# A decoder trunk in fp32 on one core: the sums of the seven-product steps get other homes in SBUF

## The chip, the cores and the metric

The kernel runs on one core of a Trainium2 chip. The metric is device time in microseconds (us). The engines named below are PE (matrix products into PSUM), DVE and ACT (elementwise work), POOL (elementwise work and the accumulating DMAs) and SP (which issues most DMAs).

## The reference

The reference is one layer of a hybrid decoder: RMS norm, one input projection, retention heads and mLSTM heads, an output projection, and then a gated ConvFFN with a final norm. Only the ConvFFN's second half is touched here:

```python
    u = rmsnorm(h, norm_ffn)
    up = causal_dwconv(u @ w_up.astype(u.dtype), ffn_conv_w, ffn_conv_b)
    gate, val = jnp.split(up, [FFN_DIM], axis=-1)
    return h + (jax.nn.silu(gate) * val) @ w_down.astype(h.dtype)
...
    h = rmsnorm(h, norm_final)
    return h[:, N_META:]
```

There are 256 tokens, a model width of 2048 and an inner width of 5632. Everything is float32.

## The kernel before

**Products.** PE takes each float32 operand as two parts: `whi`, a rounded copy that ACT makes (the cast in L121 or L764), and `wlo`, the rest, a subtraction on DVE (L123 or L766). A product is three matmuls: hi x hi, hi x lo and lo x hi.

**Halves.** The inner width is cut into two halves of 22 blocks of 128. For each half the kernel first runs the up projection: block by block two products (gate and value), then a convolution of three taps (`conv3`: `cu` in L680, three terms, the tiles `gt` and `vt`), silu and the product (L788). The results are kept split in `mh`/`ml` (plain steps) and `sh`/`sl` (fast steps). Then follows the down stage: 11 steps q of 256 inner rows, once for the first pair of column blocks of 512 (b = 0) and once for the second pair (b = 2).

**Plain steps and sevens.** Steps 0, 4, 9 and 10 are plain: per column block one load of raw weights (`load_w`, L118), a cast, a subtraction, and 12 matmuls of 128x512. The others are sevens: the two token blocks and two column blocks make a 2x2 product that is done with seven products instead of eight. A seven reads one block `kept`, made ahead of time, and three raw blocks (`wd7`) into one of two homes in `hT` (L840, L841); DVE makes three sums, two in `ta` (L844) and one in `tb` (L845); each is split (L764, L766); 21 matmuls follow (L859 to L862).

**The ring of raw weights.** `wraw` is a ring of 4 tiles of 4 KB per partition in the pool `wpool`. Each plain load takes one of its tiles, and each seven takes two, one for `ta` and one for `tb` (of which half is used). A tile comes free when its `wlo` has been made.

**Where b = 0 gives way to b = 2.** The sevens' results lie in four PSUM tiles `mmps`, the plain ones' and some of the sevens' in four tiles `atps` (`cs`). After the last seven of b, `share` puts `mmps` together: ACT copies p1 to x1 (L884), and DVE makes x6, x7, x6 again and x5 (L886, L887, L889, L895). Four DMAs on POOL's queue (L878, in `onto`) add x1, x7, x6 and x5 to the blocks (0, b), (1, b), (0, b+1) and (1, b+1) of `hn`. After the last step ACT copies the four `cs` tiles (L951) to x tiles, in the order (0, b), (1, b), (0, b+1), (1, b+1), and four more DMAs add these to the same blocks of `hn`. The x tiles are x_tile(0) to x_tile(4): x6, x7, x5 and x1 are tiles 0 to 3; the four copies go to tiles 4, 3, 1 and 0. So the second copy overwrites x1, the third x7 and the fourth x6, each once its accumulate has landed. The next pair's `cs` tiles are the same PSUM banks in the same order, so b = 2's matmuls into its n-th tile (L827 first) wait for the n-th copy.

**What sets the order.** The program is written as loops; a scheduler puts each engine's instructions in order, by its own estimates of times and by when tiles come free. Each engine runs its own list in that order. The pools `wk2` (`cu`, `gt`, `vt`; two buffers of the latter two) and `up` are given up before half 1's down stage, and the pool `more` is opened over their place.

Of the kernel before, what the change touches and what calls it, by code (L numbers as in the profile page):

```python
# [10 lines left out]
F32 = mybir.dt.float32  # L11
F32R = mybir.dt.float32r
AF = mybir.ActivationFunctionType
ALU = mybir.AluOpType
PSUM = bass.MemoryType.PSUM

P = 128
DM = 2048
KT = DM // P
SEQ = 256  # L20
# [9 lines left out]
NF = FFN // P  # L30
# [53 lines left out]
def trunk(ctx: ExitStack, tc: tile.TileContext, io, out: bass.AP):  # L84
    nc = tc.nc

    def pool(name, bufs, **kw):
        return tc.tile_pool(name=name, bufs=bufs, **kw)

    consts = ctx.enter_context(pool("consts", 1, side="left"))  # L90
    wpool = ctx.enter_context(pool("wpool", 1, side="left"))
# [10 lines left out]
    def pcol(name, i, n=1):  # L102
        a = _COLS[name][0]
        return par[:, a + i : a + i + n]
# [34 lines left out]
    def project(src, xh, xl, t0, ps=None):  # L139

        if ps is None:
            ps = mm.tile([P, 512], F32, name="mmps")
        for half in range(2):
            half_tile(ps[:, : xh(0).shape[1] - t0], src, half, xh, xl, t0)
        return ps
# [60 lines left out]
    with pool("sq", 1, side="right") as sqp:  # L206
        for k0, k1 in [(0, 1), (1, 2)] + [(k, k + 2) for k in range(2, KT, 2)]:
            n = k1 - k0
# [3 lines left out]
            raw = wpool.tile([P, 2, W0], F32, name="wraw", bufs=4)[:, :n, :]  # L212
# [5 lines left out]
            for k in range(k0, k1):  # L218
                nc.scalar.activation(xh[:, k, :], hT[:, k, :], AF.Copy, scale=pcol("gmix", k))
                nc.vector.scalar_tensor_tensor(out=xl[:, k, :], in0=hT[:, k, :], scalar=pcol("gmix", k),  # L220
                                               in1=xh[:, k, :].bitcast(F32), op0=ALU.mult, op1=ALU.subtract)
# [47 lines left out]
    with tc.issue_after(parted.ins):  # L269
        a = _COLS["retn"][0]  # L270
        nc.vector.tensor_scalar(out=norms[:, :RH], in0=par[:, a : a + RH], scalar1=-0.5, scalar2=None, op0=ALU.mult)

        a = _COLS["mln"][0]
# [295 lines left out]
    wk2 = wk2_cm.__enter__()  # L569
# [27 lines left out]
    S1, S2, S3, S4, A11, A12, A22 = range(7)  # L597
# [55 lines left out]
    def norm2():  # L653
        ms2 = at.tile([P, 512], F32, name="atps")
        nc.tensor.matmul(ms2[:, :NQ], inv_dm, ssq, start=True, stop=True)
        r0, rt = x_tile(0), x_tile(1)
        r = rsqrt_m2(r0, rt, ms2[:, :NQ], NQ, squared)
        nc.vector.tensor_scalar(out=rstd2, in0=r[:, :NQ], scalar1=-0.5, scalar2=None, op0=ALU.mult)
# [8 lines left out]
    def x_tile(i):  # L667
        return x5[:, i, :]
# [5 lines left out]
        for t in range(2):  # L674
            nc.vector.transpose(dst[:, :, t, 32 * i : 32 * (i + 1)], src[:, :, t, a, :])

    def conv3(ps, f, name):
        u = wk2.tile([P, NQ], F32, name="cu", bufs=1)
        nonlocal evacuated
        evacuated = nc.vector.tensor_tensor(out=u, in0=ps[:, :NQ], in1=rstd2, op=ALU.mult)  # L680
        o = wk2.tile([P, SEQ], F32, name=name)
        nc.scalar.activation(o, u[:, 2:], AF.Identity, scale=pcol("fw", 3 * f + 2), bias=pcol("fb", f))
        for j in range(2):
            nc.vector.scalar_tensor_tensor(out=o, in0=u[:, j : j + SEQ], scalar=pcol("fw", 3 * f + j), in1=o, op0=ALU.mult, op1=ALU.add)
        return o
# [6 lines left out]
    def squares(tt, i, c0, c1):  # L692

        nc.scalar.activation(junk[:, : c1 - c0], hn[:, tt, c0:c1], AF.Square, scale=DM ** -0.5, accum_out=ss4[:, tt, i : i + 1])
# [49 lines left out]
    for half in range(2):  # L744
# [18 lines left out]
        def split(hi, lo, x, after=None):  # L763
            copied = nc.scalar.copy(hi, x)  # L764
            with tc.issue_after(after.ins) if after else nullcontext():
                return copied, nc.vector.tensor_tensor(out=lo, in0=x, in1=hi.bitcast(F32), op=ALU.subtract)  # L766

        gt = None
        for jj in range(NHF):
            j = half * NHF + jj  # L770
            pair = []
            for s in range(2):
                pair.append(project(io["wu"][2 * j + s], uh, ul, 0))
                if j == 0 and s == 0:
                    norm2()
                for e in running:
                    e.age += 1
                if running and running[0].age == 2:
                    running.pop(0).finish(evacuated)
                if 2 * jj + s in begins:  # L780
                    n = begins.index(2 * jj + s)
                    b, q = units[n]
                    running.append(Early(b, half * NQD + q, homes[n], gt, pace))
                    early[b, q] = running[-1].kept
            gt = conv3(pair[0], j, "gt")
            vt = conv3(pair[1], NF + j, "vt")
            nc.scalar.activation(gt, gt, AF.Silu)
            nc.vector.tensor_tensor(out=gt, in0=gt, in1=vt, op=ALU.mult)  # L788
            q, i = divmod(jj, 2)
            if q in PLAIN:  # L790
                k = 2 * PLAIN.index(q) + i
                copied, parted = split(mh[:, k, :], ml[:, k, :], gt)
            elif i == 0:
                f = FAST.index(q)
                even = gt
                copied, parted = split(sh[:, f, A11, :], sl[:, f, A11, :], gt[:, 0:P])
            else:
                e11, e21, e12, e22 = even[:, 0:P], even[:, P:], gt[:, 0:P], gt[:, P:]
                if half == 1 and q in BOTH:
                    split(*(a[:, BOTH.index(q), :] for a in a21), e21)  # L800
                sums = x_tile(0).rearrange("p (a t) -> p a t", a=4)
                nc.gpsimd.tensor_tensor(out=sums[:, S1, :], in0=e21, in1=e22, op=ALU.add)
                nc.gpsimd.tensor_tensor(out=sums[:, S3, :], in0=e11, in1=e21, op=ALU.subtract)
                nc.gpsimd.tensor_tensor(out=sums[:, S2, :], in0=sums[:, S1, :], in1=e11, op=ALU.subtract)
                nc.gpsimd.tensor_tensor(out=sums[:, S4, :], in0=e12, in1=sums[:, S2, :], op=ALU.subtract)
                split(sh[:, f, A12:, :], sl[:, f, A12:, :], gt.rearrange("p (a t) -> p a t", a=2))
                copied, parted = split(sh[:, f, 0:4, :], sl[:, f, 0:4, :], sums)
            if 2 <= j < 18:
                with tc.issue_after(parted.ins):
                    transposed_h((j - 2) // 4, (j - 2) % 4)  # L810
# [21 lines left out]
        def seven(b, q, cs, ps, first, last, after, norm):  # L832


            nonlocal turn
            f = FAST.index(q)
            raw = left[turn]
            turn = 1 - turn

            nc.sync.dma_start(raw[:, 0, :], early[b, q])  # L840
            nc.sync.dma_start(raw[:, 1:4, :], io["wd7"][b // 2, half * NQD + q][:, 1:4, :])  # L841
            ta, tb = (wpool.tile([P, 2, 512], F32, name="wraw", bufs=4) for _ in range(2))

            nc.vector.tensor_tensor(out=ta, in0=raw[:, 0:1, :].to_broadcast([P, 2, 512]), in1=raw[:, 1:3, :], op=ALU.subtract)  # L844
            nc.vector.tensor_tensor(out=tb[:, 0, :], in0=raw[:, 3, :], in1=raw[:, 0, :], op=ALU.subtract)  # L845
            copied = None
            for w, to in (
                (raw[:, 2:4, :], ((S4, cs[0, 1], False, False), (A12, cs[0, 0], False, False))),
                (raw[:, 0:2, :], ((S2, ps[2], first, last), (A11, ps[0], first, last))),
                (ta, ((S3, ps[1], first, last), (S1, ps[3], first, last))),  # L850
                (tb[:, 0:1, :], ((A22, cs[1, 0], False, False),)),
            ):
                hi = wpool.tile([P, 2, 512], F32R, name="whi", bufs=5)
                lo = wpool.tile([P, 2, 512], F32R, name="wlo", bufs=5)
                n = len(to)
                with tc.issue_after(after.ins) if first and after else nullcontext():
                    copied, _ = split(hi[:, :n, :], lo[:, :n, :], w)
                for i, (m, o, begin, _) in enumerate(to):
                    nc.tensor.matmul(o, sh[:, f, m, :], hi[:, i, :], start=begin, stop=False)  # L859
                    nc.tensor.matmul(o, sl[:, f, m, :], hi[:, i, :], start=False, stop=False)  # L860
                for i, (m, o, _, end) in enumerate(to):
                    nc.tensor.matmul(o, sh[:, f, m, :], lo[:, i, :], start=False, stop=end)  # L862
            if norm:

                with tc.issue_after(copied.ins):
                    for g in norm:
                        squares(*g)
                reached = nc.gpsimd.tensor_tensor(out=junk[:, 0:1], in0=tb[:, 0, 0:1], in1=tb[:, 0, 0:1], op=ALU.add)
                with tc.issue_after(reached.ins):
                    for tt, _, c0, c1 in norm:  # L870
                        times_gain(tt, c0, c1)
# [30 lines left out]
        if half == 1:  # L902
# [3 lines left out]
            more = more_cm.__enter__()  # L906
            gfin = more.tile([P, DM], F32, name="gfin", bufs=1)
            nc.gpsimd.dma_start(gfin, io["gfin"])
            junk = more.tile([P, 512], F32, name="junk", bufs=1)
# [7 lines left out]
        for b in (0, 2):  # L917
            cs = {}
# [3 lines left out]
            ps = [mm.tile([P, 512], F32, name="mmps") for _ in range(4)]  # L922
# [38 lines left out]
        if half == 1:  # L961
# [10 lines left out]
            for i in range(2):  # L972
                p = at.tile([P, 512], F32, name="atps")[:, 0:256]
# [95 lines left out]
```

## Time and profile before

| | us |
|---|---|
| median of 3 runs | 1208.73 (1208.54 to 1211.33) |
| profiled execution | 1207.7 |
| its span | 1205.9 |
| PE busy in the span | 1194.6 |
| DVE busy | 971.5 |
| ACT busy | 709.5 |
| POOL busy | 162.8 |

Times in rows count from the start of the span. Half 0's down stage runs from 718 to some 830 us, half 1's from 1084 to the end. In both, b = 0 gives way to b = 2 at the step where L951 stands: at 773 and at 1140 us. A row of the timeline gives the start, the length, the engine, the line, the operation with its tiles, and in brackets how long the engine had been idle and what released it. A row of waits gives who waited for whom: microseconds in total, times, the longest.

### The profile page before, as it was taken

To read this page: it belongs to the slowest core of one execution; us is meant where nothing else is said; L and a number is where in the kernel's file an instruction comes from. 1 tells how busy PE (TensorE), PEld (TensorE's weight loads), DVE (VectorE), ACT (ScalarE), POOL (GpSimd) and SP (SyncE) were. 2 spreads that over 40 slices of the span, in tenths; PEclk is the share of its full clock that TensorE was granted. 3 is DMA by queue.
4 is the path that set the end of the run, shared out by engine and by line. 5 is a ranking of instruction groups with operands and counts; after the bars stand their busy time and mean duration, and the time that the engine had idled before them with its cause. 6 is when DMAs were issued, how large, how long until landed. Compare 5 with 4: busy or idle time off the path is not lost.

```text
span 1205.9 us, 22794 instructions
## 1 busy us (share of the span) xinstructions
PE 1194.6 (99%) x8956; PEld 1151.2 (95%) x8956; DVE 971.5 (81%) x1444; ACT 709.5 (59%) x963; POOL 162.8 (14%) x223
## 2 busy tenths in 40 slices
PE   9999999999999999999999999999999999999997
PEld 9999999999999999999999998878999999998886
DVE  8968788766775966789889879897788778789897
ACT  8747656655656646555555557664555555556664
POOL 0100001111110311021122100202022112100232
PEclk9999999999999999999999999999999999999999
DMA  8765555666565965766766834959787777755956
GB/s 278 269 212 164 170 184 170 197 183 192 169 192 165 349 200 175 252 220 212 253 219 214 279 117 175 278 177 276 284 251 255 223 240 249 261 176 211 274 181 186
DMA packets 83004, 263.27 MB, mean 218 GB/s; under 512 B 14672, under 2 KB 18896, under 8 KB 82768
## 3 DMA queue, kind: packets, MB, share of 16 engines
q1 hardware_dynamic: 71952, 223.85, 57.0%
q0 software_dynamic: 10368, 37.11, 10.1%
q8 instruction: 70, 1.15, 0.4%
q10 hardware_dynamic: 576, 0.85, 0.2%
q14 instruction: 38, 0.31, 0.1%
HBM read 243.42 MB, written 11.27 MB: 211 GB/s over the span
## 4 chain that ended last, share of the span: by engine, by line
PE 96%; DMA 2%; DVE 1%; ACT 0%; issue 0%; SPq 0%; DVEq 0%; ACTq 0%
PE mmps L130 26%; PE mmps L131 25%; PE mmps L133 25%; PE atps L827 2%; PE atps L828 2%; PE atps L830 2%; PE mmps L860 2%; PE mmps L862 2%; PE mmps L859 2%; PE atps L862 1%; PE atps L860 1%; PE atps L859 1%; DMA hn<-x 1%; PE atps L379 1%; DMA hT<-in_wd 1%; PE atps L371 0%
## 5 line engine op out<-in xcount | busy, mean ns | idle before, releaser
L121 ACT CAST whi<-wraw 128x1024 fp32r<-128x1024 f32 x352 | 369.3, 1050 | 342.0 <-PE mmps L131 228.7
L123 DVE TENSOR_TENSOR wlo<-wraw,whi 128x1024 fp32r<-128x1024 f32 x352 | 432.3, 1230 | 72.5 <-ACT whi L121 70.0
L130 PE MATMUL mmps<-uh,whi 128*128 128x258 f32 x1408 | 346.1, 283 | 0.0
L131 PE MATMUL mmps<-ul,whi 128*128 128x258 f32 x1408 | 346.0, 283 | 0.0
L130 PEld LDWEIGHTS mmps<-uh,whi 128*128 128x128 f32 x1408 | 267.6, 190 | 0.1
L131 PEld LDWEIGHTS mmps<-ul,whi 128*128 128x128 f32 x1408 | 267.1, 190 | 0.1
L130 PE MATMUL mmps<-xh,whi 128*128 128x272 f32 (+2 forms) x864 | 219.8, 288 | 0.0
L131 PE MATMUL mmps<-xl,whi 128*128 128x272 f32 (+2 forms) x864 | 218.3, 286 | 0.0
L133 PE MATMUL mmps<-uh,wlo 128*128 128x258 f32 x1408 | 196.5, 282 | 0.0
L133 PEld LDWEIGHTS mmps<-uh,wlo 128*128 128x128 f32 x1408 | 179.9, 189 | 0.0
L131 PEld LDWEIGHTS mmps<-xl,whi 128*128 128x128 f32 x864 | 162.8, 188 | 0.0
L130 PEld LDWEIGHTS mmps<-xh,whi 128*128 128x128 f32 x864 | 162.5, 188 | 0.1
L133 PE MATMUL mmps<-xh,wlo 128*128 128x272 f32 (+2 forms) x864 | 126.7, 285 | 0.0
L133 PEld LDWEIGHTS mmps<-xh,wlo 128*128 128x128 f32 x864 | 114.2, 188 | 0.0
L680 DVE TENSOR_TENSOR cu<-mmps,rstd 128x258 f32<-128x258 f32 x88 | 37.4, 425 | 55.3 <-PE mmps L133 54.8
L764 ACT CAST whi<-hT 128x1024 fp32r<-128x1024 f32 x52 | 53.6, 1052 | 27.2 <-PE atps L828 7.3
L766 DVE TENSOR_TENSOR wlo<-hT,whi 128x1024 fp32r<-128x1024 f32 x52 | 62.1, 1220 | 4.9 <-ACT whi L764 3.7
L131 PE MATMUL mmps<-mixl,whi 128*128 128x258 f32 x256 | 63.0, 283 | 0.0
L130 PE MATMUL mmps<-mixh,whi 128*128 128x258 f32 x256 | 62.4, 282 | 0.0
L764 ACT CAST whi<-wraw 128x1024 fp32r<-128x1024 f32 (+1 forms) x52 | 43.0, 838 | 16.8 <-PE mmps L860 6.8
L766 DVE TENSOR_TENSOR wlo<-wraw,whi 128x1024 fp32r<-128x1024 f32 (+1 forms) x52 | 52.2, 1037 | 0.6 <-PE mmps L862 0.2
L827 PE MATMUL atps<-whi,mh 128*128 128x512 f32 (+1 forms) x132 | 50.9, 387 | 1.3 <-ACT whi L121 1.1
(280 smaller groups left out, 1700.1 us busy)
## 6 DMA issues: line engine op xcount, KB each, us to landing
wraw<-in_wu SPq DMA_DIRECT2D x176, 512.0 KB, 4.4
wraw<-in_wi SPq DMA_DIRECT2D x108, 512.0 KB, 4.1
hT<-in_wd SPq DMA_DIRECT2D x26, 768.0 KB, 4.7
wraw<-in_wd SPq DMA_DIRECT2D x36, 512.0 KB, 4.7
wraw<-in_wo SPq DMA_DIRECT2D x32, 512.0 KB, 4.2
x<-in_wd POOLq DMA_DIRECT2D x13, 768.0 KB, 7.0
hn<-x POOLq DMA_DIRECT2D x27, 256.0 KB, 7.9
hT<-kept SPq DMA_DIRECT2D x26, 256.0 KB, 2.9
```

The source lines that it names most:

```text
L121: nc.scalar.copy(hi, raw)
L123: nc.vector.tensor_tensor(out=lo, in0=raw, in1=hi.bitcast(F32), op=ALU.subtract)
L130: nc.tensor.matmul(ps, hi[:, k, :], xh(kk), start=kk == first, stop=False)
L131: nc.tensor.matmul(ps, hi[:, k, :], xl(kk), start=False, stop=False)
L133: nc.tensor.matmul(ps, lo[:, k, :], xh(kk), start=False, stop=kk == last)
L680: evacuated = nc.vector.tensor_tensor(out=u, in0=ps[:, :NQ], in1=rstd2, op=ALU.mult)
L764: copied = nc.scalar.copy(hi, x)
L766: return copied, nc.vector.tensor_tensor(out=lo, in0=x, in1=hi.bitcast(F32), op=ALU.subtract)
L827: nc.tensor.matmul(ps, ah[i], hi[:, i, cols], start=first and i == 0, stop=False)
L859: nc.tensor.matmul(o, sh[:, f, m, :], hi[:, i, :], start=begin, stop=False)
L860: nc.tensor.matmul(o, sl[:, f, m, :], hi[:, i, :], start=False, stop=False)
L862: nc.tensor.matmul(o, sh[:, f, m, :], lo[:, i, :], start=False, stop=end)
```

## The change

In half 0 a seven takes one tile of the ring, for `ta`. `tb` goes to a tile `both`, which holds what used to be `gt` and `vt` side by side, also with two buffers. In half 1 `ta` and `tb` go to tiles of their own in the pool `more`, with two buffers each (12 KB more in all), and a seven takes nothing from the ring.

```diff
-    def conv3(ps, f, name):
+    def conv3(ps, f, o):
...
-        o = wk2.tile([P, SEQ], F32, name=name)
...
-            gt = conv3(pair[0], j, "gt")
-            vt = conv3(pair[1], NF + j, "vt")
+            both = wk2.tile([P, 2, SEQ], F32, name="both")
+            gt = conv3(pair[0], j, both[:, 0, :])
+            vt = conv3(pair[1], NF + j, both[:, 1, :])
...
-            ta, tb = (wpool.tile([P, 2, 512], F32, name="wraw", bufs=4) for _ in range(2))
+            if half == 0:
+                ta = wpool.tile([P, 2, 512], F32, name="wraw", bufs=4)
+                tb = wk2.tile([P, 2, SEQ], F32, name="both").rearrange("p a t -> p (a t)")
+            else:
+                ta, tb = more.tile([P, 2, 512], F32, name="ta"), more.tile([P, 512], F32, name="tb")
...
-            nc.vector.tensor_tensor(out=tb[:, 0, :], in0=raw[:, 3, :], in1=raw[:, 0, :], op=ALU.subtract)
+            nc.vector.tensor_tensor(out=tb, in0=raw[:, 3, :], in1=raw[:, 0, :], op=ALU.subtract)
...
-                (tb[:, 0:1, :], ((A22, cs[1, 0], False, False),)),
+                (tb.rearrange("p (a n) -> p a n", a=1), ((A22, cs[1, 0], False, False),)),
...
-                reached = nc.gpsimd.tensor_tensor(out=junk[:, 0:1], in0=tb[:, 0, 0:1], in1=tb[:, 0, 0:1], op=ALU.add)
+                reached = nc.gpsimd.tensor_tensor(out=junk[:, 0:1], in0=tb[:, 0:1], in1=tb[:, 0:1], op=ALU.add)
```

Lines from L764 on have other numbers now: L844, L845 are L848, L849; L878 is L882; L884, L886, L887, L889, L895 are L888, L890, L891, L893, L899; L951 is L955. Since the scheduler sees other tiles, it also puts instructions in another order. Three places follow.

POOL, where b = 0 gives way to b = 2 in half 0: the eight accumulates into `hn`, with the semaphores that each waits for. DMASW stands for the landing of an earlier DMA of POOL, Activation for a copy on ACT, DVE for a result of share. Before:

```order
L878 DMA hn<-x_5849 128x512 [waits DVE_49,Activation_49]
L878 DMA hn<-x_5849 128x512 [waits DVE_49]
L878 DMA hn<-x_5849 128x512 [waits DVE_49,Pool_49]
L878 DMA hn<-x_5849 128x512 [waits DVE_49]
L878 DMA hn<-x_5849 128x512 [waits DMASW4_49,Activation_49]
L878 DMA hn<-x_5849 128x512 [waits DMASW5_49,Activation_49]
L878 DMA hn<-x_5849 128x512 [waits DMASW6_49,Activation_49]
L878 DMA hn<-x_5849 128x512 [waits DMASW7_49,DMASW3_49,Activation_49]
```

and now:

```order
L882 DMA hn<-x_5849 128x512 [waits DVE_49,Activation_49]
L882 DMA hn<-x_5849 128x512 [waits DVE_49]
L882 DMA hn<-x_5849 128x512 [waits DMASW4_49,Activation_49]
L882 DMA hn<-x_5849 128x512 [waits DMASW5_49,Activation_49]
L882 DMA hn<-x_5849 128x512 [waits DVE_49,Pool_49]
L882 DMA hn<-x_5849 128x512 [waits DVE_49]
L882 DMA hn<-x_5849 128x512 [waits DMASW0_49,Activation_49]
L882 DMA hn<-x_5849 128x512 [waits DMASW3_49,DMASW1_49,Activation_49]
```

Before, x1, x7, x6 and x5 come first (the first four rows) and the four copies' accumulates after them. Now the first two copies' accumulates stand third and fourth, each waiting for a landing (x1's and x7's), and x6 and x5 behind them. In half 1 the eight rows have moved in the same way.

DVE, half 1, from the splits of b = 0's last seven to x5. Here `ta`, `tb` and `wraw<-hT` are sums of sevens, `wlo<-wraw` by L123 the splits of plain steps, and `x<-mmps` the rows of share. Before:

```order
L766 TENSOR_TENSOR wlo<-wraw,whi 128x512
L123 TENSOR_TENSOR wlo<-wraw,whi 128x1024 x2
L886 TENSOR_TENSOR x_5849<-mmps,x_5849 128x512
L887 TENSOR_TENSOR x_5849<-mmps,x_5849 128x512
L889 TENSOR_TENSOR x_5849<-x_5849,mmps 128x512
L895 TENSOR_TENSOR x_5849<-x_5849,mmps 128x512
```

and now:

```order
L765 TENSOR_TENSOR wlo<-tb,whi 128x512
L848 TENSOR_TENSOR ta<-hT 128x1024
L849 TENSOR_TENSOR tb<-hT 128x512
L123 TENSOR_TENSOR wlo<-wraw,whi 128x1024 x3
L890 TENSOR_TENSOR x_5849<-mmps,x_5849 128x512
L123 TENSOR_TENSOR wlo<-wraw,whi 128x1024
L848 TENSOR_TENSOR ta<-hT 128x1024
L849 TENSOR_TENSOR tb<-hT 128x512
L891 TENSOR_TENSOR x_5849<-mmps,x_5849 128x512
L123 TENSOR_TENSOR wlo<-wraw,whi 128x1024 x2
L893 TENSOR_TENSOR x_5849<-x_5849,mmps 128x512
L899 TENSOR_TENSOR x_5849<-x_5849,mmps 128x512
```

x7 (L887, now L891) stood two rows behind the splits of step 9; now the sums of two later sevens and two more splits of plain steps stand ahead of it. In half 0 it is the same with one `ta`, one `tb` and two splits.

SP, half 0, the loads for the second pair from step 3's seven to step 6's. Before:

```order
L840 DMA hT<-kept_3_7228 128x512
L841 DMA hT<-in_wd 128x1536
L840 DMA hT<-kept_5_7514 128x512
L841 DMA hT<-in_wd 128x1536
L118 DMA wraw<-in_wd 128x1024 x2
L840 DMA hT<-kept_6_7806 128x512
```

and now:

```order
L840 DMA hT<-kept_3_7219 128x512
L841 DMA hT<-in_wd 128x1536
L840 DMA hT<-kept_5_7503 128x512
L118 DMA wraw<-in_wd 128x1024 x2
L841 DMA hT<-in_wd 128x1536
L840 DMA hT<-kept_6_7793 128x512
```

The two loads of plain step 4 (L118) have moved ahead of the L841 row of step 5's seven, and they no longer wait for a tile that a seven holds.

## The prediction

> **What bounds the kernel now.** I read the head of the page first, then what PE waits for over the whole span, then ten-microsecond windows of the two down stages.
>
> ```profile
> span 1205.9 us, 22794 instructions
> PE 1194.6 (99%) x8956; PEld 1151.2 (95%) x8956; DVE 971.5 (81%) x1444; ACT 709.5 (59%) x963; POOL 162.8 (14%) x223
> ```
> ```profile
> PE atps L827 <- ACT whi L121: 1.1, 2, 0.7
> ...
> PE atps L827 <- ACT x L951: 0.2, 1, 0.2
> ```
> ```profile
> 790.00:800.00 10.00, 9.55 (x42) 7.52 (x41) 10.00 (x11) 6.42 (x7) 0.00 (x0) 1.00 0.55 206
> ...
> 810.00:820.00 10.00, 9.35 (x41) 7.38 (x40) 9.91 (x11) 5.30 (x6) 0.00 (x0) 1.00 0.33 109
> ...
> 1140.00:1150.00 10.00, 9.84 (x44) 8.08 (x44) 8.34 (x9) 8.82 (x12) 3.50 (x4) 1.00 1.01 235
> ```
> PE has work 99% of the span. In the down stages it waits three times: twice for the cast of a plain step's weights (L121) and once for a copy that empties a PSUM tile (L951). The windows show the price (columns: time, length, then busy time of PE, PEld, DVE, ACT, POOL): 0.45, 0.65 and 0.16 us are missing. Measured as the start to start of matmuls over their usual 0.23 us, the gaps come to 0.7, 0.9 and 0.4 us, because the matmul after each gap is slower too. So nothing in these stages can win more than 2.0 us. A loss has no such limit, so the places to look at are those where PE has little margin.
>
> **The gain: two weight loads come earlier.** The two L121 waits belong to steps 4 and 9 of half 0's second pair of column blocks (b = 2). Their loads sit in SP's queue until a seven gives back its ring slots:
>
> ```profile
> 783.43 0.42 SPq L841 DMA_DIRECT2D hT<-in_wd  x1
> 788.90 0.93 SPq L118 DMA_DIRECT2D wraw<-in_wd  x2
> ```
> The load of step 4 is issued at 788.9, although the row ahead of it is done at 783.9. With one slot per seven, SP has these two loads directly behind the L840 row of that moment, with no wait on a tb: some 5 us earlier, against a wait of 0.7. Step 9's pair likewise waits for the sums of a seven earlier. I count both gaps as gone: -0.7 - 0.9 = -1.6 us. Instruction counts are unchanged on every engine; tb's subtraction and its split cost the same in another tile.
>
> **The loss: the order on POOL where b = 0 gives way to b = 2.** Here the scheduler has moved more than the diff says. At this place POOL issues eight accumulating DMAs into hn: four from share (x1, x7, x6, x5) and four from the copies of the PSUM tiles, each of which must wait for the share's accumulate into the same block of hn. Before, share's four stand together:
>
> ```profile
> 763.86 0.92 POOL L878 DMA_DIRECT2D hn<-x  x1 [83.33 <-ACT x L884]
> 766.03 2.77 POOL L878 DMA_DIRECT2D hn<-x  x3 [1.25 <-DVE x L887]
> 773.79 3.52 POOL L878 DMA_DIRECT2D hn<-x  x4 [4.99 <-ACT x L951]
> ```
> ```profile
> 1129.28 0.88 POOL L878 DMA_DIRECT2D hn<-x  x1 [44.04 <-ACT x L884]
> 1131.13 2.76 POOL L878 DMA_DIRECT2D hn<-x  x3 [0.96 <-DVE x L887]
> ```
> Now the order on POOL is x1, x7, then the copies' accumulates into blocks (0, b) and (1, b), and only then x6 and x5. The one into (1, b) waits for x7 to land, and x6 stands behind it in the queue. The fourth copy (L951, L955 now) writes the tile that x6 is read from, so it waits for x6 to land; and b = 2's fourth PSUM tile is free only after that copy. A chain of two landings in a row has come into being: x7's DMA, landing, one POOL issue, x6's DMA, landing, copy, PE. That POOL does hold its queue for a landing shows in its waits, once in this run:
>
> ```profile
> POOL hn L878 <- DMA hn<-x: 1.4, 1, 1.4
> ```
> [...]
>
> Besides, x7 itself is made later. Its DVE row (L887, now L891):
>
> ```profile
> 764.25 0.68 DVE L886 TENSOR_TENSOR x<-mmps,x 128x512 f32<-128x512 f32 x1
> 765.03 0.69 DVE L887 TENSOR_TENSOR x<-mmps,x 128x512 f32<-128x512 f32 x1
> ...
> 768.55 1.23 DVE L844 TENSOR_TENSOR wraw<-hT 128x1024 f32<-128x1024 f32 x1
> 769.69 2.35 DVE L123 TENSOR_TENSOR wlo<-wraw,whi 128x1024 fp32r<-128x1024 f32 x2
> ```
> ```profile
> 1076.17 1.22 DVE L844 TENSOR_TENSOR wraw<-hT 128x1024 f32<-128x1024 f32 x1
> ...
> 1080.26 0.69 DVE L845 TENSOR_TENSOR wraw<-hT 128x512 f32<-128x512 f32 x1
> ...
> 1084.79 1.22 DVE L766 TENSOR_TENSOR wlo<-wraw,whi 128x1024 fp32r<-128x1024 f32 x1
> ...
> 1127.08 2.36 DVE L123 TENSOR_TENSOR wlo<-wraw,whi 128x1024 fp32r<-128x1024 f32 x2 [0.44 <-PE atps L862]
> 1129.36 0.69 DVE L886 TENSOR_TENSOR x<-mmps,x 128x512 f32<-128x512 f32 x1
> 1130.13 0.69 DVE L887 TENSOR_TENSOR x<-mmps,x 128x512 f32<-128x512 f32 x1
> ```
> A row of 128x1024 takes 1.14 us from start to start (768.55 to 769.69), one of 128x512 about 0.6 (0.69, less the same overlap). In half 0 a tb, two splits and a ta now stand ahead of x7 behind the two splits of step 9: 0.6 + 3 x 1.14 = 4.0 us. So x7's DMA goes out at 766.0 + 4.0 = 770.0. In half 1 two ta, two tb and two splits more stand ahead of it: 4 x 1.14 + 2 x 0.6 = 5.8, less the idle 0.44: 5.3. To that comes a lead that DVE loses at the start of half 1: ta, tb and ta's split of the first seven (1076.17, 1080.26, 1084.79; 2.9 us together) ran there before the last convolution was done, and now stand behind it. Bounds: none of it is still felt (5.3), or all of it (8.2). DVE has only some 0.8 us of idle time in view to absorb it, so I take 2.1, and x7's DMA goes out at 1131.1 + 7.4 = 1138.5.
>
> When PE needs the tiles, and what a copy takes:
>
> ```profile
> 776.50 0.39 PE L827 MATMUL atps<-whi,mh 128*128 128x512 f32 x1
> ...
> 777.87 0.39 PE L827 MATMUL atps<-whi,mh 128*128 128x512 f32 x1
> ```
> ```profile
> 1140.19 0.50 PE L827 MATMUL atps<-whi,mh 128*128 128x512 f32 x1 [0.16 <-ACT x L951]
> ...
> 1144.42 0.39 PE L827 MATMUL atps<-whi,mh 128*128 128x512 f32 x1
> ```
> ```profile
> 772.92 2.25 ACT L951 COPY x<-atps 128x512 f32<-128x512 f32 x4
> ```
> PE starts b = 2's fourth tile at 777.87 and at 1144.42. The copy is 0.6 us. With L for the landing of x7 and M for that of x6, 0.9 for the POOL issue between them (0.92 for one above), 0.6 for the copy and 0.1 for the hand-overs, PE can go on at 771.6 + L + M in half 0 and 1140.1 + L + M in half 1. The stalls are **L + M - 6.3** and **L + M - 4.3**.
>
> Landings, from asking for the issue to hn at 763.9, at 766.0, at 773.8, at 1131.1 and at 1140.4, and the page's median:
>
> ```profile
> DMA to landing us min/median/max: 8.2/8.2/8.2
> ...
> DMA to landing us min/median/max: 7.1/7.1/7.1
> ...
> DMA to landing us min/median/max: 4.4/4.4/4.4
> ...
> DMA to landing us min/median/max: 6.1/6.1/6.1
> ```
> ```profile
> hn<-x POOLq DMA_DIRECT2D x27, 256.0 KB, 7.9
> ```
> ```profile
> 760.48 4.21 SPq L118 DMA_DIRECT2D wraw<-in_wd  x4
> 778.53 0.33 SPq L840 DMA_DIRECT2D hT<-kept  x1
> ...
> 1125.73 15.53 SPq L118 DMA_DIRECT2D wraw<-in_wd  x6
> ```
> The ones that go out beside weight loads take 7 to 8 us (8.2 at 763.9 and at 1131.1, 7.1 at 766.0); the one at 773.8, where SP issues nothing from 764.7 to 778.5, takes 4.4. In half 0 x7 at 770.0 falls into that lull: L = 5.0, and M = 5.1, a little over the 4.4 because two more go out with it. Stall 3.8 us; bounds 2.5 (4.4 twice) and 8.1 (7.1 and 7.3). In half 1 SP issues loads until 1141.3, so L = 8.2 as x7's own row there; x6 at 1147.6 comes after them: M = 5.5. Stall 9.4; bounds 2.4 (4.4 twice, x7 only 5.3 late) and 13.1 (8.2, 8.4, x7 8.2 late).
>
> [...]
>
> Other moves cost nothing as far as I can walk them: half 1's first seven has its ta cast about 2 us before PE wants it, and behind the last copy the first cast (1.05 us) ends within the six matmuls (1.4 us) that PE still has.
>
> **Sum.** 3.8 + 9.4 - 1.6 = +11.6 us. Against the profiled execution's own 1207.7 (span 1205.9 and 1.8 around it) that is 1219.3. The median of the runs is 1.0 higher, so I predict **1220 us**.
>
> **Rivals.** *The accumulates stay hidden.* If L + M is under 6.3 in half 0 and under 4.3 in half 1, no copy is late, the change does just what it says, and the time is 1208.7 - 1.6 = 1207.1, not slower. For it: 0.2 us is all that copies cost PE now. Against it: every landing quoted is 4.4 or more, so half 1 would have to land both in less than one takes today. 5%. [...] 3%. *Landings as long as beside loads, in both halves*: 8.1 + 13.1 - 1.6 = +19.6, 1228; decided if the issue at 770.0 takes over 7 us. 15%. *DVE's lost lead stalls PE as well at the start of half 1*: if ta's cast there comes over 2 us later than I walk it, PE waits up to the 2.9 us that were moved, 1223. 10%. *My chain, 1213 to 1225*: 65%. The remaining 2% is for a gain that I do not see.
>
> **How the numbers follow.** The bounds give 2.5 + 2.4 - 1.6 = +3.3 and 8.1 + 13.1 - 1.6 = +19.6, or 1212 to 1228; I take 1213 to 1229, since casts behind the copies have only 0.3 us of margin and can add something at the upper end. A change of 0.3%, 3.6 us, is about what a measurement here tells from none. Slower by more: 15 + 10 + 65 = 0.90. Within it, the first two rivals: 0.08. Faster: 0.02, since PE's gaps hold only 2.0 us.
>
> **What would show it.** In the profile after: PE waits for copies of L955 in both halves, before the third and fourth tile of b = 2, of 2 to 8 us in half 0 and 5 to 13 in half 1; POOL's x6 accumulate goes out some 8 us after x7's instead of 1; the two L121 waits are gone; POOL waits for its own hn<-x. I am wrong if POOL shows share's four accumulates together, or if PE has no wait on L955, or if landings in these places are under 4 us.

## The result, and the profile after

The changed kernel takes 1225.0 us in the median (1224.09 to 1226.85), the kernel before 1209.4 beside it (1208.54 to 1211.33): a ratio of 1.0138, with a 95% interval of 1.0126 to 1.015. The change makes the kernel some 16 us slower. The profiled execution took 1226.85 us, 19.15 more than the profiled one before; that is the pair of executions which the accounting below splits up, and it lies 3.5 us further apart than the medians.

The head of the page:

```profile
span 1225.1 us, 22795 instructions
PE 1200.4 (98%) x8956; PEld 1154.1 (94%) x8956; DVE 969.2 (79%) x1444; ACT 706.2 (58%) x963; POOL 167.3 (14%) x223
```

DVE and ACT are busy a little less than before, POOL 4.5 us more, which is still only 14% of the span. PE is busy for 5.8 us more with the same 8956 matmuls, so some of them were slower. The rest of the 19 us has to be waiting. What PE and POOL wait for (us in total, times, the longest):

```profile
PE atps L827 <- ACT x L955: 10.4, 4, 3.7
...
PE mmps L866 <- DVE wlo L765: 0.3, 1, 0.3
```
```profile
POOL hn L882 <- DMA hn<-x: 12.0, 5, 4.8
```

The two waits for a plain step's cast (L121) are gone. In their place PE waits 10.4 us for the copies out of PSUM (L955, formerly L951, 0.2 us), and POOL holds its queue for 12.0 us until its own accumulates have landed (1.4 before). POOL's row of issues shows where, in half 0 and in half 1:

```profile
773.25 0.88 POOL L882 DMA_DIRECT2D hn<-x  x1 [6.31 <-DVE x L891]
775.41 0.86 POOL L882 DMA_DIRECT2D hn<-x  x1 [1.28 <-ACT x L955]
776.99 2.63 POOL L882 DMA_DIRECT2D hn<-x  x3 [0.72 <-DMA hn<-x]
782.88 0.86 POOL L882 DMA_DIRECT2D hn<-x  x1 [3.25 <-DMA hn<-x]
...
1144.44 0.88 POOL L882 DMA_DIRECT2D hn<-x  x1 [6.96 <-DVE x L891]
1146.25 0.85 POOL L882 DMA_DIRECT2D hn<-x  x1 [0.93 <-ACT x L955]
1151.88 2.61 POOL L882 DMA_DIRECT2D hn<-x  x3 [4.78 <-DMA hn<-x]
```

The first row of each is x7, the second the copies' accumulate into (0, b), the group of three the one into (1, b) with x6 and x5 behind it. In half 1 x7 is issued at 1144.44, and after one more issue POOL stands still until it has landed. x6, which has nothing to do with that landing, goes out some 8 us after x7 instead of one. ACT's copies wait for both landings in turn:

```profile
1145.38 1.06 ACT L955 COPY x<-atps 128x512 f32<-128x512 f32 x2
1151.45 0.58 ACT L955 COPY x<-atps 128x512 f32<-128x512 f32 x1 [5.00 <-DMA hn<-x]
1156.79 0.58 ACT L955 COPY x<-atps 128x512 f32<-128x512 f32 x1 [4.75 <-DMA hn<-x]
```

And PE behind them, in its own rows of both halves:

```profile
775.17 0.50 PE L827 MATMUL atps<-whi,mh 128*128 128x512 f32 x1 [0.70 <-ACT x L955]
...
783.06 0.79 PE L827 MATMUL atps<-whi,mh 128*128 128x512 f32 x1 [3.15 <-ACT x L955]
783.65 0.63 PE L828 MATMUL atps<-whi,ml 128*128 128x512 f32 x1
784.08 0.63 PE L827 MATMUL atps<-whi,mh 128*128 128x512 f32 x1
784.50 0.63 PE L828 MATMUL atps<-whi,ml 128*128 128x512 f32 x1
...
789.66 0.39 PE L863 MATMUL mmps<-whi,sh 128*128 128x512 f32 x1
789.89 0.39 PE L864 MATMUL mmps<-whi,sl 128*128 128x512 f32 x1
...
1152.09 0.50 PE L827 MATMUL atps<-whi,mh 128*128 128x512 f32 x1 [2.91 <-ACT x L955]
...
1157.42 0.50 PE L827 MATMUL atps<-whi,mh 128*128 128x512 f32 x1 [3.69 <-ACT x L955]
```

A second cost shows here. After the wait of 3.15 us the matmuls start 0.43 us apart (783.65 to 784.08 to 784.50) until about 789.2; then they are 0.23 apart again (789.66 to 789.89). From 783.06 to 789.19 there are 14 of them where 0.23 us each would make 3.2 us: 2.9 us are lost after the wait is over. After the wait at 1157.42 ten matmuls lose 1.7 us. The windows have it as PEclk, the granted clock (the last three columns are PEclk, the DMA share and GB/s):

```profile
780.00:790.00 10.00, 6.94 (x18) 5.46 (x19) 5.30 (x6) 6.54 (x8) 1.72 (x2) 0.66 0.84 195
790.00:800.00 10.00, 10.00 (x46) 8.19 (x45) 9.24 (x10) 7.49 (x9) 0.00 (x0) 1.00 0.73 252
```

**Where the 19 us are.** The two kernels have the same matmuls in nearly the same order, so the start of the n-th can be compared. After minus before, step by step: -0.2 us up to the down stage of half 0; +0.75 ahead of its hand-over, where a seven's splits come late (L866 in the waits above); +7.55 at its hand-over from b = 0 to b = 2; -1.7 at the two earlier loads of plain steps; +8.3 at the hand-over of half 1; +0.8 from there to the last matmul, where the matmuls start a little further apart than before (why is not shown); and +3.7 in the stretch from the last matmul to the end, which took 8.2 us before and 11.9 now. Sum 19.2, for the 19.15 measured. Of the two hand-overs, 10.45 us are waits (0.70 + 3.15 + 2.91 + 3.69) and 4.6 slow matmuls (2.9 + 1.7); the rest is mostly the slower first matmul after a wait (0.50 us long at 775.17, 1152.09 and 1157.42 and 0.79 at 783.06, for 0.39).

The longer end comes from the same place in the last block. DVE's rows of share there:

```profile
1197.82 0.68 DVE L890 TENSOR_TENSOR x<-mmps,x 128x512 f32<-128x512 f32 x1
1199.77 1.22 DVE L123 TENSOR_TENSOR wlo<-wraw,whi 128x1024 fp32r<-128x1024 f32 x1 [1.27 <-ACT whi L121]
1200.91 0.68 DVE L891 TENSOR_TENSOR x<-mmps,x 128x512 f32<-128x512 f32 x1
1202.37 1.23 DVE L123 TENSOR_TENSOR wlo<-wraw,whi 128x1024 fp32r<-128x1024 f32 x1 [0.77 <-ACT whi L121]
1203.51 0.68 DVE L893 TENSOR_TENSOR x<-x,mmps 128x512 f32<-128x512 f32 x1
1204.11 0.68 DVE L899 TENSOR_TENSOR x<-x,mmps 128x512 f32<-128x512 f32 x1
```

Splits of the last plain loads stand between them and wait for casts, so x5 is ready at 1204.8. Before, splits stood there too, but none waited:

```profile
1185.05 1.22 DVE L123 TENSOR_TENSOR wlo<-wraw,whi 128x1024 fp32r<-128x1024 f32 x1
1186.18 0.68 DVE L889 TENSOR_TENSOR x<-x,mmps 128x512 f32<-128x512 f32 x1
1186.78 0.68 DVE L895 TENSOR_TENSOR x<-x,mmps 128x512 f32<-128x512 f32 x1
```

By the last matmul's clock x5 is 1.9 us later than before, and its accumulate lands in 5.3 us, for 3.3 before. It stands in the chain that ends last (start, length, what):

```profile
1205.08 5.28 DMA hn<-x
1210.39 0.69 DVE hn L904
```

### The profile page after: what moved, and what is told of

Same layout as the page of the kernel before. It is cut to its first block, busy times and chain, and to the rows that moved or that the text cites. A ratio compares the mean times of both kernels' runs of the same rounds, so it can differ in the third digit from the quotient of the medians.

```text
span 1225.1 us, 22795 instructions
## 1 busy us (share of the span) xinstructions
PE 1200.4 (98%) x8956; PEld 1154.1 (94%) x8956; DVE 969.2 (79%) x1444; ACT 706.2 (58%) x963; POOL 167.3 (14%) x223
## 4 chain that ended last, share of the span: by engine, by line
PE 94%; DMA 3%; DVE 1%; issue 1%; ACT 1%; POOL 0%; SPq 0%; DVEq 0%; ACTq 0%; POOLq 0%
PE mmps L130 25%; PE mmps L131 25%; PE mmps L133 25%; DMA hn<-x 2%; PE mmps L863 2%; PE mmps L864 2%; PE mmps L866 2%; PE atps L827 2%; PE atps L828 2%; PE atps L830 2%; PE atps L863 1%; PE atps L864 1%; PE atps L866 1%; PE atps L379 1%; DMA wraw<-in_wd 0%
## 5 line engine op out<-in xcount | busy, mean ns | idle before, releaser
L121 ACT CAST whi<-wraw 128x1024 fp32r<-128x1024 f32 x352 | 367.4, 1049 | 286.3 <-PE mmps L131 182.2
L123 DVE TENSOR_TENSOR wlo<-wraw,whi 128x1024 fp32r<-128x1024 f32 x352 | 432.0, 1231 | 68.5 <-ACT whi L121 66.8
L683 DVE SCALAR_TENSOR_TENSOR both<-cu,par,both 128x256 f32<-128x256 f32 x176 | 84.7, 481 | 6.4 <-ACT both L681 4.2
L681 ACT ACTIVATE both<-cu,par 128x256 f32<-128x256 f32 x88 | 53.0, 602 | 45.0 <-DVE cu L680 32.3
L827 PE MATMUL atps<-whi,mh 128*128 128x512 f32 (+1 forms) x132 | 52.0, 395 | 10.5 <-ACT x L955 10.4
```

Source lines behind the costliest of these rows:

```text
L121: nc.scalar.copy(hi, raw)
L123: nc.vector.tensor_tensor(out=lo, in0=raw, in1=hi.bitcast(F32), op=ALU.subtract)
L827: nc.tensor.matmul(ps, ah[i], hi[:, i, cols], start=first and i == 0, stop=False)
```

## The experiments

Each kernel was timed against the kernel before on the same chip; ratios are to that, with 95% intervals. "Before" had medians of 1207.0 to 1207.6 us there.

### Is POOL's order enough by itself?

The theory: x6 and x5 behind the first two copies' accumulates make two landings in a row. The rival: it is DVE, which makes x7 later, and POOL's order hardly matters. The first kernel takes the changed one and gives share's four accumulates back their place on POOL; the second takes the kernel before, whose DVE order and ring are untouched, and moves only x6 and x5 behind the two copies' accumulates.

```diff
-                        onto(tt, b + j, x)
+                        with tc.issue_after(shared.ins):     # share's last accumulate
+                            onto(tt, b + j, x)
```

> The changed kernel, but on POOL's queue the accumulates of the four copies are put behind the four of share, in both halves; every result is the same and the order on DVE stays as the change made it. Theory A (the hand-over from b = 0 to b = 2 costs the time, because x7 and x6 are added late): x6's DMA goes out right after L893 instead of after x7's landing. In the changed kernel it went out at 777.9 with L893 done at 776.9 (half 0: at most 0.9 us to win) and at 1152.8 with L893 done at 1147.3 (half 1: up to 5 us to win, less a longer landing beside others). So 3 to 6 us faster than the changed kernel, 1219 to 1222 us. If POOL's order were the main cause, as the prediction had it, 10 us or more would come back: below 1215. Theory B (the new homes themselves cost the time, through DVE's lost lead, and the order of accumulates only shows it): no change, 1224 to 1226.

Measured: 1219.1 us, 1.0092 (1.0078 to 1.0106). What PE waits for:

```profile
PE atps L827 <- ACT x L955: 6.2, 4, 2.0
```

The waits fall from 10.4 to 6.2 us, the longest from 3.7 to 2.0, and no stretch of slow matmuls follows any of them. But 12 us of the 16 remain: with POOL's order mended, x7 and x6 are still made late by DVE, and the copies wait for their landings all the same. By the n-th matmul the two hand-overs still cost 7.1 us, where the changed kernel loses 15.8; the last block and the end cost 4.4.

```diff
             else:
-                onto(0, b + 1, x6)
+                pass
...
-            onto(1, b + 1, x5)
+            if final:
+                onto(1, b + 1, x5)
...
-                        onto(tt, b + j, x)
+                        added = onto(tt, b + j, x)
+                        if (j, n) == (0, 1):
+                            with tc.issue_after(added.ins):
+                                onto(0, b + 1, x_tile(0))
+                                onto(1, b + 1, x_tile(2))
```

> The kernel before the change (both sums in the ring), but on POOL's queue x6 and x5 stand behind the accumulates of the first two copies, as the changed kernel has them; DVE makes x7 and x6 as early as before. This prices POOL's order alone. In the profile of before the second copy ends at 774.2 (half 0) and 1140.7 (half 1); then one issue of 0.9, x6's landing of 4.1 to 6, the fourth copy of 0.6: PE goes on at some 780.5 and 1147.5 where it needed 777.9 and 1144.4. Theory A1 (POOL's order costs by itself, the prediction's step): two waits of 1.5 to 3 us, 3 to 6 us slower than before. Theory A2 (the order on DVE is what costs, POOL's order only with it): under 1 us.

Measured: 1222.5 us, 1.0119 (1.0101 to 1.0137). PE's waits, and POOL's issues in half 1:

```profile
PE atps L827 <- ACT x L952: 9.3, 3, 5.1
```
```profile
1135.81 0.89 POOL L878 DMA_DIRECT2D hn<-x  x1 [0.97 <-DVE x L887]
1144.67 3.49 POOL L878 DMA_DIRECT2D hn<-x  x4 [7.98 <-ACT x L952]
1153.73 0.86 POOL L878 DMA_DIRECT2D hn<-x  x1 [5.57 <-issue]
```

Here x7 is as early as before (1135.81) and has landed when the copies come, 8 us later. One landing is left, x6's, which can only start when the copies do. That alone costs 14.9 us: waits of 3.8 and 5.1 us, a short one of 0.4, slow matmuls behind the two long ones, and 2.3 us more in the last block and at the end. The 3 to 6 us that were expected are missed by more than double: x6's landing took 6.0 and 7.5 us, and the slow matmuls and the end were not in the sum. So POOL's order is a sufficient cause, and so, nearly, is DVE's (e1). The two don't add up: both lead to the wait of the fourth copy for x6.

### Each half alone

> Only half 0 has the new homes; in half 1 the sums lie in the ring as before. Theory A: half 0's share of the loss alone. In the changed kernel half 0's down stage came out 6.6 us longer by its matmuls (8.3 lost where b = 0 gives way to b = 2, 1.7 won by the two earlier loads), so 1209.4 + 6.6 = 1216, plus or minus 1.5, with the last matmul to the end of the span as before (8.5 us, not 12.2). Theory B: half 0 has free room in the convolution's place and loses nothing of itself, 1208 to 1210.

> Only half 1 has the new homes; in half 0 both sums lie in the ring as before. Theory A: half 1's share of the loss alone: 8.3 us where b = 0 gives way, 0.8 by a slower PE after that, 3.7 at the end of the span, so 1209.4 + 12.8 = 1222, less what was due to half 0; 1219 to 1223. The two gaps of half 0 (0.7 and 0.9 us) are back. Theory B: the same, or all of the loss (1225), since half 1's homes lie over the convolution's pool.

Each takes the changed kernel and gives the other half's `ta` and `tb` back to the ring (the first by the two lines here, the second by the same lines in the other branch):

```diff
-                ta, tb = more.tile([P, 2, 512], F32, name="ta"), more.tile([P, 512], F32, name="tb")
+                ta, tb = (wpool.tile([P, 2, 512], F32, name="wraw", bufs=4) for _ in range(2))
+                tb = tb[:, 0, :]
```

Measured: half 0 alone 1212.5 us, 1.0044 (1.0028 to 1.0059); half 1 alone 1218.8 us, 1.0095 (1.0081 to 1.0108). PE's waits, first of half 0 alone, then of half 1 alone:

```profile
PE atps L827 <- ACT x L956: 2.4, 1, 2.4
```
```profile
PE atps L827 <- ACT x L955: 5.5, 2, 2.9
...
PE atps L827 <- ACT whi L121: 1.1, 2, 0.6
```

Both halves lose on their own, 5.3 and 11.6 us, and the sum is 16.9 for the 15.6 of the whole change. With half 1 alone the two L121 waits are back at 1.1 us, as before: they belong to half 0's new homes. The longer end of the span (11.15 us from the last matmul, for 8.2) is half 1's; half 0 alone has 8.25.

### Both orders written out: what is left of the gain?

Now both reorderings are undone by hand, and the new homes stay. If the theory is whole, the loss goes and the 1.6 us of the earlier loads stay. Written out in three places: the sums of b = 2's sevens and the splits of step 10 stand behind share's last DVE row, and the copies' accumulates behind share's last accumulate.

```diff
+            with tc.issue_after(shared[0].ins) if b else nullcontext():
                 nc.vector.tensor_tensor(out=ta, ...)
                 nc.vector.tensor_tensor(out=tb, ...)
...
-                    w = load_step(b + j, q)
+                    w = load_step(b + j, q, after=shared[0] if q == steps[-1] and not final else None)
...
-                        onto(tt, b + j, x)
+                        with tc.issue_after(shared[1].ins):
+                            onto(tt, b + j, x)
```

> The changed kernel with its new homes, and three orders written down: the sums of b = 2's sevens and the splits of step 10 are queued on DVE behind share's last row, and on POOL the copies' accumulates behind share's four. Nothing else is changed. Theory A: x7 and x6 are added as early as before the change, the copies are not late, and of the change only the gain is left: 1209.4 - 1.7 = 1207.7, 1206.5 to 1209.5, no wait on L955 of over 0.3 us. Theory B: the homes cost what they cost, 1218 or more, with waits of PE on casts or splits.

Measured: 1211.4 us, 1.0034 (1.0021 to 1.0046): the loss shrinks from 16 to 4 us, but no gain. PE's waits:

```profile
PE mmps L868 <- DVE wlo L766: 1.9, 2, 1.0
```

No wait for a copy is left, and none for L121. By the n-th matmul this kernel is 2.0 us ahead of the kernel before until half 1's hand-over and 2.2 us ahead after it. Of this, 0.25 us were there before the down stages began and have nothing to do with the change. So the gain is there, and of the size that was worked out: 1.7 us for the two loads. Then it loses 3.1 us in the last block (b = 2 of half 1), and the stretch from the last matmul to the end takes 10.6 us. The same three orders with half 0's homes alone, where that last block is as before:

> New homes in half 0 alone, half 1's sums in the ring as before, and the three written orders of the fourth experiment in both halves. If what was left of the loss there (4 us) comes from half 1's homes (the last block, where DVE waited for raw blocks, and the end of the span), it is gone here, and the gain of the two earlier loads is left: 1.7 to 2.2 us faster than before, ratio 0.998. If it comes from the written orders, some 4 us slower, ratio 1.003.

Measured: 1206.9 us against 1207.6, 0.9996 (0.9987 to 1.0005): no difference that can be told from none. A gain of 1.6 us would be 0.9987, the lower end of the interval; whether a part of it is there stays open, since the profile taken is that of the longest run (1210.6 us) and can't be read for the median.

Who holds the last block? DVE waits there for raw blocks of sevens (`hT`) and in turn makes splits late. Two more orders are added: a seven's sums stand behind the splits of the raw blocks of the seven ahead of it, and then also the splits of the last plain loads behind share's rows.

```diff
+            ... tc.issue_after(behind.ins) if behind and not first else nullcontext():    # around ta and tb
+                if to[0][0] == S2:
+                    behind = parted
```

> The fourth experiment (new homes in both halves, three written orders) with one order more: on DVE the sums of a seven are queued behind the splits of the raw blocks of the seven ahead. In the fourth experiment's last block DVE took up sums first whose raw block had not landed and idled 2.75, 1.05 and 0.75 us there, and PE waited for splits twice for 1.0 us. If that order is the cause, these waits go and 3 us come back: ratio 1.001, with the longer end of the span (10.6 against 8.2 us) still there. If the late raw blocks come from the loads that the free ring lets ahead of them, the idle time only moves: ratio 1.003 as before.

```diff
-                ws[q] = load_step(3, q, more if n % 2 else wpool)
+                ws[q] = load_step(3, q, more if n % 2 else wpool, shared[0])
```

> The seventh experiment with one order more: in the last block the splits of the last loads stand behind share's rows on DVE, which waited there behind splits of late loads. If that is what made the end of the span longer (10.5 us from the last matmul to the end, 8.2 before), 2 us come back: ratio 1.000 to 1.001. The two waits of PE for splits in the last block (1.0 and 0.9 us) stay, since they have another cause: DVE, which ends the last seven's splits at 1177.7 in the seventh experiment and at 1177.5 before. If the end is longer for another reason, ratio 1.002 as in the seventh.

Measured: the first 1209.97 us, 1.002 (1.0011 to 1.0028), with the end still at 10.5 us. Less than 2 us come back, not 3, and PE's two waits for splits stay (1.7 us, for 1.9), so they have another cause than the order of the sums. With the second order 1207.4 us, 1.0004 (0.9995 to 1.0013), and the end is back at 8.2 us. That settles the longer end: it was the splits between share's rows, which wait for casts. What is still given back is 1.7 us in the last block: ahead by 1.6 us at half 1's hand-over, behind by 0.1 at the last matmul. DVE's rows there, of the kernel with the second order, and POOL's beside them:

```profile
1172.72 2.35 DVE L766 TENSOR_TENSOR wlo<-hT,whi 128x1024 fp32r<-128x1024 f32 x2
1174.99 2.32 DVE L766 TENSOR_TENSOR wlo<-ta,whi 128x1024 fp32r<-128x1024 f32 x1
1177.24 0.68 DVE L766 TENSOR_TENSOR wlo<-tb,whi 128x512 fp32r<-128x512 f32 x1
```
```profile
1173.94 2.29 POOL L698 TENSOR_TENSOR hn<-hn,gfin 128x512 f32<-128x512 f32 x1
```

DVE has no idle time between these rows, and the split at 1174.99 takes 2.32 us instead of 1.2. It starts while POOL multiplies by the final norm's gain (1173.94 to 1176.23) and ends 1.1 us after that. Next, these multiplications are left out, with the written orders and, for comparison, in the kernel before (part of the final norm's gain is then missing from the output):

> The kernel of the eighth experiment without the multiplications by the final gain that POOL does within the sevens of the last block (part of the final norm's gain is left out). In the last block some DVE rows of 128x1024 take 2.2 to 2.3 us in place of 1.2, once for each of these. If DVE bounds the last block, so that what was won earlier (2.2 us by the matmuls) is given back there, the two waits of PE go, and this kernel is 1.5 to 2.5 us faster than the tenth, which leaves out the same in the kernel before. If DVE's long rows are not due to POOL, or do not set PE's waits, the two are equal within 1 us.

> The kernel before the change without the same multiplications. PE had no wait in its last block, so nothing to win there: within 1 us of before, ratio 0.999 to 1.001, but DVE's rows of 2.2 to 2.9 us in the last block are gone.

Measured: 1206.2 us, 0.9989 (0.998 to 0.9998), against 1207.1 us, 1.0004 (0.9994 to 1.0014) for the kernel before without them. The long rows are gone in the first, the split above among them, and PE has no wait in the last block:

```profile
1174.09 1.22 DVE L766 TENSOR_TENSOR wlo<-ta,whi 128x1024 fp32r<-128x1024 f32 x1
```

By the n-th matmul it is 1.0 us ahead both at half 1's hand-over and at the last matmul, where the kernel of e8 gave back 1.7. In the kernel before the multiplications cost nothing that shows. This is what a last block bound by DVE would show, but the times alone would not prove it: the two medians are 0.9 us apart, where 1.5 to 2.5 were expected and up to 1 was the rival's number, and the two intervals overlap. Can the multiplications be had elsewhere? Last, they are moved behind share's last accumulate:

```diff
-                reached = nc.gpsimd.tensor_tensor(out=junk[:, 0:1], in0=tb[:, 0:1], in1=tb[:, 0:1], op=ALU.add)
-                with tc.issue_after(reached.ins):
-                    for tt, _, c0, c1 in norm:
-                        times_gain(tt, c0, c1)
+                later.extend(norm)
...
+                            with tc.issue_after(shared[1].ins):
+                                for tt, _, c0, c1 in later:
+                                    times_gain(tt, c0, c1)
```

> The kernel of e8 with the multiplications by the final norm's gain on POOL (which stretched VectorE's splits from 1.2 to 2.2-2.3 us inside the last block's sevens) moved behind the share's last accumulate; nothing is left out. If the last block is bound by VectorE only because of those multiplications, the gain of the earlier loads (about 2.3 us by the third stage's hand-over of half 1) shows at the end as in the kernel that leaves them out: 0.9985 of before, a span about 1.8 us below that of before, no wait of TensorE in the last block. The rival: the multiplications stretch the last splits there as well, or hold up the norm's end, by as much: 1.000 to 1.002, with VectorE rows over 2 us behind the share's last row or a tail over 9 us from the last matmul to the end.

Measured: 1208.9 us, 1.001 (1.0001 to 1.0019), the rival's number. DVE's row there, POOL's beside it, and PE's wait:

```profile
1181.67 7.36 DVE L124 TENSOR_TENSOR wlo<-wraw,whi 128x1024 fp32r<-128x1024 f32 x2
```
```profile
1182.61 5.33 POOL L698 TENSOR_TENSOR hn<-hn,gfin 128x512 f32<-128x512 f32 x4
```
```profile
PE atps L831 <- DVE wlo L124: 2.4, 1, 2.4
```

Two splits take 7.36 us instead of 2.35 beside four multiplications, and PE, 2.1 us ahead until then, ends 1.0 behind. The multiplications cost DVE much the same in both places: 5.0 us for four here, 1.1 for the one beside the split at 1174.99 in e8. No version with the whole output came out faster than the kernel before by more than the noise.

## Why the prediction was right, point by point

The forecast was 1220 us within 1213 to 1229; the median is 1225.0. The mechanism was right. That the number came so near is in part luck: the stalls were priced 2.75 us too high, some 10 us of the profiled pair's difference were not priced, and the medians lie 3.5 us closer together than that pair.

**PE bound, at most 2.0 us to win.** Right in kind. With the loss taken away, PE gets at most 2.3 us ahead (e7, at half 1's hand-over; 0.15 of it from before the down stages), and nothing of it reaches the end, which the prediction didn't say: the last block is bound by DVE's splits, not by PE's work.

**The two earlier loads, -1.6.** Right for the step itself: -1.7 in the profile, and both waits for L121 gone. The changed kernel's profile is no proof of the cause, since its PE comes to these steps some 8 us late, and in e5, late by 6.4 us with the old ring, the two gaps are gone by 1.7 us as well. But e4 is not late there and has the same -1.7, and e3, with the old ring in half 0, has both waits. What they are worth is less sure than one profile made it: 1.1 us of waits in the two executions of before and e3, but 0.5 in e10, whose ring is that of the kernel before.

**The order on POOL.** Confirmed by the trace and by e5. The prediction took the chain for one of two landings; e5 shows that x6's alone, begun only when the copies are done, is enough for 15 us.

**x7 made later on DVE.** In half 1 right: predicted at 1138.5 on the clock of before, measured at 1144.44 with PE 6.4 us behind by then, 1138.0; with half 1 alone, 1137.62. So the walk over the DVE rows, and the 2.1 us taken for the lost lead, held. In half 0 it was 3.25 us too early (770.0, measured 773.25). The step missed DVE's lateness ahead of that place. A raw block for a seven came later, first before, then after:

```profile
747.74 1.23 DVE L844 TENSOR_TENSOR wraw<-hT 128x1024 f32<-128x1024 f32 x1 [0.78 <-DMA hT<-in_wd]
```
```profile
750.79 1.23 DVE L848 TENSOR_TENSOR wraw<-hT 128x1024 f32<-128x1024 f32 x1 [2.13 <-DMA hT<-in_wd]
...
767.64 0.69 DVE L849 TENSOR_TENSOR both<-hT 128x512 f32<-128x512 f32 x1 [0.66 <-DMA hT<-in_wd]
```

DVE is 3.05 us late at the first of them. The plain loads that now go out early stand ahead of the sevens' blocks on SP; the prediction booked only their benefit. That this order on SP is the cause was read from the rows, not tried.

**L and M.** Both too long: x7 landed in 3.2 and 6.9 us (5.0 and 8.2 assumed), x6 in 4.6 and 4.3 (5.1 and 5.5). From asking for x7's issue and for the group with x6 in half 1, where x6 is the middle one of three:

```profile
DMA to landing us min/median/max: 6.9/6.9/6.9
...
DMA to landing us min/median/max: 3.5/4.3/5.1
```

**The stalls.** 3.8 and 9.4 predicted; PE waited 3.85 and 6.60. Half 0 is right by luck, by errors that cancel: x7 came 3.25 us later, the landings were 1.8 + 0.5 shorter, and PE itself was 0.6 later. Half 1 follows from x7's issue and the landings: 9.4 - 0.5 - 1.3 - 1.2 = 6.4.

**What the sum lacked.** Two terms: the slow matmuls after the waits, 4.6 us, and the longer end, 3.7 us. For the end there were rows to walk: share stands in the last block too, with splits between its rows, and only the hand-overs were walked. "Other moves cost nothing" is the step that failed. The slow matmuls had no row in the profile before, where the waits in the down stages are 0.7 us at most.

**The rivals.** "They stay hidden" falls with the waits. The 3% beside it belong to a time for a landing that no run shows: the shortest landing that PE stood behind took 3.2 us. The lost lead of DVE at the start of half 1 stalled nothing there. Long landings in both halves did not occur, though 1225 lies between that case and the forecast for another reason, the slow matmuls and the end.

## What to carry to other kernels

A buffer that is short also keeps a schedule in order: where it is made larger, look first at what the scheduler pulls ahead, on the DMA queue, on the engine that prepares operands and on the queue of accumulates, and put back by hand the orders on which a hand-over rests. An issue that waits for a landing should stand last on its queue, behind all that need not wait (POOL held its queue for 12.0 us here). And a gain upstream counts only if the last block can take it: here the 2 us won were lost to an engine that PE had hidden before.

## What the runs showed of the hardware

**A wait of PE can cost a second time.** After waits of 2.4 us (e2), 2.9 and 2.6 (e3), 3.15 and 3.7 (after) and 3.8 and 5.1 (e5) matmuls start 0.427 us apart, for 0.229 otherwise, and the granted clock of a 10 us window falls as low as 0.66 (after, 780 to 790). No slow stretch follows waits of up to 2.0 us (e1), nor the one of 2.9 us at 1152.09 in the changed kernel. So the length of the wait does not decide it alone.

In the changed kernel's trace the granted clock is at half twice before the last matmul: from 782.35 to 789.18 and from 1157.82 to 1161.23. These four times lie 2, 110 and 1 times 3.41 us apart. Counted from them, the span is taken in windows of 3.41 us. PE stands idle for 2.44 us of the window ahead of the first drop (778.94 to 782.35) and for 3.02 us of the one ahead of the second (1154.40 to 1157.82). In every other window before the last matmul it is idle for 1.81 us at most, and no drop follows. The wait that ends at 1152.09 lies across an edge: the windows on its two sides have 1.81 and 1.76 us idle. Two drops in one trace are an observation, not a rule, and what makes the clock drop is not shown.

**DVE's splits took longer beside POOL's multiplications.** A split of 128x1024 at the same place took 1.22 us with the multiplications left out (e9, 1174.09) and 2.32 us where it started during one (e8, 1174.99). The latter ended 1.1 us after POOL's row (1173.94 to 1176.23), which is about one split's length. Two splits took 7.36 us beside four multiplications (e11, 1181.67), for 2.35 without. What holds DVE up inside is not shown by these rows.
